# Moving the delta rule's steps in a head's plan: pairs of blocks from matmul 362 to 336, the recurrence from 400 to 374, decays loaded at 62, exponentials in four steps

## The chip, the cores and the metric

The kernel runs on one core of one Trainium2 chip. The metric is the device time of one launch in microseconds (us), lower being better. The time before is 2664.57 us, the median of 3 runs (2664.34 to 2671.64).

## What is computed

A decoder trunk of two layers over 1024 tokens and 1024 features in float32. Each layer normalises x, projects it with one large matrix, runs a sparse attention branch and a gated delta rule branch on the projections, and adds the gated mixture of the two, projected once more, to x. The part that matters here is the delta rule, for each of 8 heads, in chunks (of 64 tokens in the reference, of 128 in the kernel):

```python
decay = exp(where(incl, gc[..., :, None] - gc[..., None, :], -inf))
lower = where(strict, einsum('bhnid,bhnjd->bhnij', kb, k) * decay, 0.0)
tmat  = eye + lower
u = triangular_solve(tmat, v * beta);  w = triangular_solve(tmat, kb * exp(gc))
qk = einsum('bhnid,bhnjd->bhnij', q, k) * decay
def step(state, chunk):
    v_new = u_c - w_c @ state
    o_c   = qd_c @ state + qk_c @ v_new
    state = state * g_tot + kd_c^T @ v_new
```

q, k and v come out of a short causal convolution and a silu; the output o goes through an RMS norm and is multiplied by two gates.

## The kernel before, in words

A layer has three phases: a token phase (projections with tokens on the partitions, and the choice of keys), a feature phase (`feature_phase`, the delta rule and its gates), and attention with the output projection. Every large matmul is done as three passes over a high and a low part (`w_hi`, `w_lo`, `hi_t`, `lo_t`). The change touches the feature phase alone.

**The stream of projections.** The feature phase runs over heads 0 to 7. For each head `conv` projects k, q and v, in this order: 48 matmuls each (two halves of 24, L388). Behind each half ScalarE copies the result out (L750, L751); behind both halves VectorE does three multiply-adds of 1024 columns (L757), ScalarE a tanh (L760) and VectorE one more multiply (L761). From head 1 on, `gdn_finish` of the head before then projects two gates with 96 matmuls. So head 0 has 144 such matmuls, and each head after it 240, and `self.count` counts them over the phase (2208 in a layer, with the three gates of the attention branch that are done behind head 7's projections).

**The plan.** What is left of the delta rule is cut into small steps, and `plan_head` gives each a position: a number of projection matmuls from the head's first one. `planned` is called behind every projection matmul and emits the steps whose position has been reached. Each step's instructions are ordered behind that matmul on TensorE and behind the last evacuation (`act_last`) on ScalarE, and get a high priority; on VectorE, GpSimd and in SP's DMA queue they stand where the scheduler's order puts them. All engines run their instructions in order. A step whose data are late is moved back by the scheduler, so a position is a request. The next head starts 240 matmuls later (144 after head 0), so **position p of head h is count p − 240 of head h+1** for head 1 and later, and count p − 480 of head h+2. Head 0's positions are counts p − 144 of head 1 and p − 384 of head 2. The text below names such counts "count n".

**The steps before**, at these positions of a head:
- 80 `decays_load`: on GpSimd's queue, a DMA of 512 KB into `H` (L724), a masking sweep over it on GpSimd (affine_select, L725), then a DMA of 512 KB into `qe` (L729). `H` has two buffers, so head h+2's load waits until the last step of head h that reads `H`.
- 118 `decays_exp`: eight exponentials on ScalarE (L736).
- 100, 106 `gdn_keys`: four transposes on TensorE, a square on ScalarE (L774), a sum and a product on VectorE (L775, L787); the second half ends in a chain of small VectorE operations (L793, `rsqrt` L137 to L142, L795 to L798) that gives `g_nc`.
- 138 `gdn_row`: TensorE transposes `g_nc` (L805), ScalarE copies it (L807), and five small DMAs on SP's queue give `g_ccomp` (L809, L812).
- 142, 147 `gdn_queries`; 151 to 163 `gdn_products`: the chunks' products on TensorE (L834), each multiplied by `H` on VectorE (L836, L837); from 163 on `gdn_inverse`: DMAs out of `H` and back into `wide`, a scaling (L931), 62 small VectorE operations (L940, L942) that invert the blocks of 32, and DMAs back into `H` (L946, L949).
- 184 `qf` times `qe` (L713); 204, 210 `gdn_values`.
- 362, then every 6 matmuls: the six steps of `inverse_pairs`, which put the inverted blocks together. The first is three VectorE transposes (L959) into `xf`; the next five alternate small matmuls (L968, L975, L982, L988, L994) and their evacuations on VectorE or ScalarE, each needing the step before it.
- 400, then every 7 matmuls: the 23 steps of the recurrence, `gdn_chunks`: `g_r` (L867 on TensorE, L869 on VectorE), `g_u` (L872, then ScalarE L874), the new state `g_s` (L878, then VectorE L881 or L883) with the output (L886, L887, ScalarE L888, L890). The last read of `H` is the `g_u` of chunk 7, at position 547.
- 562 `norms` (a chain of small VectorE operations and one multiply of 1024 columns, L903 to L905) and 572, 578 `outputs` (transposes L911, a VectorE multiply L912 and a DMA each).

**One more order.** The three transposes of the pairs' first step are put behind one VectorE instruction by hand:

```python
        with self.tc.issue_after(self.convolved):     # L955; convolved is set at L757
            for b in range(3):
                nc.vector.transpose(XF[bs, :, co:co + 32], XT[bs, :, bs])
```

`self.convolved` is the last multiply-add of the latest convolution emitted by then.

Of the kernel before, what the change touches and what calls it, by code (L numbers as in the profile page):

```python
# [20 lines left out]
try:  # L21
# [10 lines left out]
OP = mybir.AluOpType  # L32
# [4 lines left out]
P = 128  # L37
S = 1024
D = 1024
T = S // P  # L40
# [29 lines left out]

AT_DECAYS, AT_EXP, AT_KEYS, AT_ROW, AT_QUERIES, AT_PRODUCTS, AT_DECAYED, AT_VALUES, AT_PAIRS, AT_CHUNKS, AT_NORMS, AT_OUTPUTS = (
    80, 118, (100, 106), 138, (142, 147), (151, 155, 159, 163), 184, (204, 210), 362, 400, 562, (572, 578))

STEP_PAIRS, STEP_CHUNKS = 6, 7

# [16 lines left out]
class Trunk:  # L94
# [207 lines left out]
    def at(self, pos, step):  # L302

        self.plan.append((pos, len(self.plan), step))
# [394 lines left out]
    def plan_head(self, p, hd, XF):  # L699

        nc = self.nc
        at = lambda pos, *steps, gap=0: [self.at(hd["at"] + pos + i * gap, f) for i, f in enumerate(steps)]
        at(AT_DECAYS, lambda: self.decays_load(p, hd))
        at(AT_EXP, lambda: self.decays_exp(hd))
        for half in range(2):
            at(AT_KEYS[half], lambda half=half: self.gdn_keys(p, hd, half))
            at(AT_QUERIES[half], lambda half=half: self.gdn_queries(hd, half))
            at(AT_VALUES[half], lambda half=half: self.gdn_values(p, hd, half))
        at(AT_ROW, lambda: self.gdn_row(p, hd))
        for i, pos in enumerate(AT_PRODUCTS):  # L710
            at(pos, lambda i=i: self.gdn_products(p, hd, 2 * i))
        at(AT_PRODUCTS[-1], lambda: self.gdn_inverse(p, hd))
        at(AT_DECAYED, lambda: nc.vector.tensor_mul(hd["qf"], hd["qf"], hd["qe"]))  # L713
        pairs = self.inverse_pairs(p, hd, XF)
        at(AT_PAIRS, *[lambda: next(pairs, None)] * 6, gap=STEP_PAIRS)
        chunks = self.gdn_chunks(p, hd)
        at(AT_CHUNKS, *[lambda: next(chunks, None)] * (3 * T - 1), gap=STEP_CHUNKS)
# [11 lines left out]
            nc.gpsimd.dma_start(out=qe.rearrange("p (t c) -> p t c", c=P),  # L729
                                in_=ap(self.rows, (T * 8 + h) * P, [[0, P], [8 * P, T], [1, P]]))  # L730

    def decays_exp(self, hd):


        for c in range(T):
            self.nc.scalar.activation(hd["H"][:, c], hd["H"][:, c], AF.Exp, bias=self.ngm[:, c, hd["h"]:hd["h"] + 1])  # L736

    def conv(self, l, p, ht, hd, name, base, bufs):

        nc = self.nc  # L740
        feat = self.feat[l]
        dst = hd[name] = p.tile([P, S], F32, name=name, bufs=bufs)
        col = base + hd["h"] * P
        cw = lambda j: feat[:, 24 * j + col // P:24 * j + col // P + 1]
        self.xps.append(self.xps.pop(0))
        xp = self.xps[0]

        def evac(hs, acc):
            o = hs.start
            nc.scalar.copy(xp[:, 4 + o:516 + o], acc)  # L750
            self.act_last = nc.scalar.activation(dst[:, hs], acc, AF.Copy, scale=cw(3)).ins  # L751

        ws = self.feat_weights(self.w_in[l], C_QKVB + col)
        for half in range(2):
            self.proj_feat(ws, half, ht, evac)
        for j in range(3):
            self.convolved = nc.vector.scalar_tensor_tensor(dst, xp[:, 1 + j:1 + j + S], cw(j), dst, op0=OP.mult,  # L757
                                                            op1=OP.add).ins
        th = xp[:, 4:4 + S]
        nc.scalar.activation(th, dst, AF.Tanh, scale=0.5)  # L760
        nc.vector.scalar_tensor_tensor(dst, th, 1.0, dst, op0=OP.add, op1=OP.mult)  # L761

    def turned(self, src, half):

# [129 lines left out]
    def gdn_finish(self, l, p, ht, hd):  # L894

        nc = self.nc
        feat = self.feat[l]
        gates = list(self.gated(l, ht, C_ZB + hd["h"] * P, C_GB + hd["h"] * P))

        def norms():  # L900
            o = hd["vb"]
            ms = self.small.tile([P, T], F32, name="g_ms")
            nc.vector.scalar_tensor_tensor(ms, hd["osq"], 1.0 / P, hd["zq"], op0=OP.mult, op1=OP.add)  # L903
            rs = self.rsqrt(ms, T)
            nc.vector.tensor_mul(o, o, rs[:, :, None].to_broadcast([P, T, P]))  # L905

        def outputs(half):
            h, b = hd["h"], gates[half]
            pt = self.tr()
            for i in range(4):  # L910
                nc.tensor.transpose(pt[:, i * P:(i + 1) * P], hd["vb"][:, 4 * half + i], self.ident)  # L911
            nc.vector.scalar_tensor_tensor(b, pt, feat[:, 96:97], b, op0=OP.mult, op1=OP.mult)  # L912
            nc.sync.dma_start(out=self.yb[h, :, 512 * half:512 * half + 512], in_=b)

        self.at(hd["at"] + AT_NORMS, norms)
        for half in range(2):
            self.at(max(hd["at"] + AT_OUTPUTS[half], self.count + 2), lambda half=half: outputs(half))
# [33 lines left out]
    def inverse_pairs(self, p, hd, XF):  # L951

        nc, nc_ = self.nc, hd["nc"]
        XT = H = hd["H"]
        with self.tc.issue_after(self.convolved):  # L955
            for b in range(3):
                bs = slice(32 * b, 32 * b + 32)
                co = 32 if b == 1 else 0
                nc.vector.transpose(XF[bs, :, co:co + 32], XT[bs, :, bs])  # L959
        yield  # L960
        ncb = lambda sl, n: nc_[sl, :, None].to_broadcast([sl.stop - sl.start, T, n])
        y2 = p.tile([P, T, 32], F32, name="y2", bufs=1)

        pairs = [(slice(32 * b, 32 * b + 32), slice(32 * b + 32, 32 * b + 64)) for b in (0, 2)]
        py = self.bank("ch")
        for c in range(T):
            for k, m in pairs:
                nc.tensor.matmul(py[m, 32 * c:32 * c + 32], H[k, c, m], XF[k, c, 0:32], start=True, stop=True)  # L968
        for k, m in pairs:
            nc.vector.tensor_mul(y2[m], py[m, :256].rearrange("p (c i) -> p c i", c=T), ncb(m, 32))  # L970
        yield
        pz = self.bank("ch")
        for c in range(T):
            for k, m in pairs:
                nc.tensor.matmul(pz[k, 32 * c:32 * c + 32], y2[m, c], XT[m, c, m], start=True, stop=True)  # L975
        for k, m in pairs:
            nc.scalar.copy(XT[k, :, m], pz[k, :256].rearrange("p (c i) -> p c i", c=T))
        yield
        m = slice(32, 64)
        pw = self.bank("ch")  # L980
        for c in range(T):
            nc.tensor.matmul(pw[m, 32 * c:32 * c + 32], XT[m, c, m], y2[m, c], start=True, stop=True)  # L982
        nc.scalar.copy(XF[m, :, 0:32], pw[m, :256].rearrange("p (c i) -> p c i", c=T))
        yield
        k, m = slice(0, 64), slice(64, 128)
        py = self.bank("ch")
        for c in range(T):
            nc.tensor.matmul(py[m, 64 * c:64 * c + 64], H[k, c, m], XF[k, c], start=True, stop=True)  # L988
        y3 = XF
        nc.vector.tensor_mul(y3[m], py[m].rearrange("p (c i) -> p c i", c=T), ncb(m, 64))  # L990
        yield
        pz = self.bank("ch")
        for c in range(T):
            nc.tensor.matmul(pz[k, 64 * c:64 * c + 64], y3[m, c], XT[m, c, m], start=True, stop=True)  # L994
        nc.scalar.copy(XT[k, :, m], pz[k].rearrange("p (c i) -> p c i", c=T))
# [252 lines left out]
```

## Time and profile before

| | |
|---|---|
| median of 3 runs | 2664.57 us (2664.34 to 2671.64) |
| the profiled execution | 2668.25 us |
| its span, first to last instruction | 2666.4 us |
| mean granted TensorE clock | 0.988 |
| TensorE busy (matmul) | 2565.7 us, 96% |
| VectorE busy | 1893.6 us, 71% |
| ScalarE busy | 1349.6 us, 51% |
| GpSimd busy | 136.1 us, 5% |
| feature phase, first layer | from 358.6 to 1066.4 us |
| feature phase, second layer | from 1675.1 to 2388.3 us |

The profile is of one execution; the sums of the prediction are made against its own 2668.25 us. A busy TensorE says that matmuls are in its pipeline, not that it works at its peak. In the rows below PE is TensorE, DVE VectorE, ACT ScalarE, POOL GpSimd, SP the queue of DMA issues. "x3" is a number of instructions, "[1.72 <-DVE ...]" the time for which the engine stood idle before the row, and what ended it.

### The profile page before, as it was taken

To read this page: it belongs to the slowest core of one execution; us is meant where nothing else is said; L and a number is where in the kernel's file an instruction comes from. 1 tells how busy PE (TensorE), PEld (TensorE's weight loads), DVE (VectorE), ACT (ScalarE), POOL (GpSimd) and SP (SyncE) were. 2 spreads that over 40 slices of the span, in tenths; PEclk is the share of its full clock that TensorE was granted. 3 is DMA by queue.
4 is the path that set the end of the run, shared out by engine and by line. 5 is a ranking of instruction groups with operands and counts; after the bars stand their busy time and mean duration, and the time that the engine had idled before them with its cause. 6 is when DMAs were issued, how large, how long until landed. Compare 5 with 4: busy or idle time off the path is not lost.

```text
span 2666.4 us, 42133 instructions
## 1 busy us (share of the span) xinstructions
PE 2565.7 (96%) x14858; PEld 2115.4 (79%) x14858; DVE 1893.6 (71%) x5086; ACT 1349.6 (51%) x3107; POOL 136.1 (5%) x382
## 2 busy tenths in 40 slices
PE   7999999999999999999999999999999999999998
PEld 7777778777888888898796777787878877878986
DVE  7677977667777853797366889776877767547965
ACT  5579734343444422797245795343444443337952
POOL 0122000000000000000001220000000000000000
PEclk9999999999999999999999999999999999999999
DMA  3122343142333323431420232422432233243233
GB/s 124 49 64 81 86 103 61 41 87 54 66 70 70 68 62 95 139 92 57 145 63 32 72 105 73 98 60 38 88 70 59 60 68 66 60 126 125 75 99 119
DMA packets 285431, 211.35 MB, mean 79 GB/s; under 512 B 72290, under 2 KB 239268, under 8 KB 285220
## 3 DMA queue, kind: packets, MB, share of 16 engines
q1 hardware_dynamic: 280612, 191.88, 25.7%
q0 software_dynamic: 4608, 16.78, 5.1%
q8 instruction: 117, 1.92, 0.3%
q14 instruction: 94, 0.77, 0.1%
HBM read 162.19 MB, written 46.40 MB: 78 GB/s over the span
## 4 chain that ended last, share of the span: by engine, by line
PE 46%; issue 20%; DVE 6%; DMA 4%; ACT 3%; POOL 1%; SPq 0%; DVEq 0%; POOLq 0%; ACTq 0%
PE acc L388 12%; PE acc L365 7%; PE more L388 5%; PE acc L1140 4%; PE wide L1108 4%; PE tr L1131 2%; PE out L365 2%; PE out L388 2%; PE tr L834 1%; ACT t_junk L596 1%; DMA H<-rows 1%; DVE t_junk L578 1%; PE wide L545 1%; DMA w_raw<-in_w_out_dram 1%; DVE scores L554 1%
## 5 line engine op out<-in xcount | busy, mean ns | idle before, releaser
L388 PE MATMUL acc<-hi_t,w_hi 128*128 128x512 f32 x1240 | 502.7, 405 | 5.6 <-DVE gate L663 5.0
L388 PE MATMUL acc<-hi_t,w_lo 128*128 128x512 f32 x1240 | 504.7, 407 | 0.0
L388 PE MATMUL acc<-lo_t,w_hi 128*128 128x512 f32 x1240 | 502.9, 406 | 0.0
L148 DVE TENSOR_TENSOR w_lo<-w_raw,w_hi 128x512 fp32r<-128x512 f32 (+1 forms) x336 | 223.6, 669 | 193.3 <-ACT w_hi L147 175.4
L147 ACT CAST w_hi<-w_raw 128x512 fp32r<-128x512 f32 (+1 forms) x336 | 201.1, 602 | 304.6 <-PE acc L388 143.4
L365 PE MATMUL acc<-w_hi,hi_t 128*128 128x512 f32 (+1 forms) x768 | 287.5, 375 | 13.7 <-ACT w_hi L147 9.0
L365 PE MATMUL acc<-w_lo,hi_t 128*128 128x512 f32 (+1 forms) x768 | 286.1, 373 | 2.2 <-DVE w_lo L148 2.2
L365 PE MATMUL acc<-w_hi,lo_t 128*128 128x512 f32 (+1 forms) x768 | 285.1, 371 | 0.0
L388 PEld LDWEIGHTS acc<-hi_t,w_hi 128*128 128x128 f32 x1240 | 234.9, 189 | 53.1 <-DVE gate L663 5.9
L388 PEld LDWEIGHTS acc<-hi_t,w_lo 128*128 128x128 f32 x1240 | 234.8, 189 | 46.4
L388 PEld LDWEIGHTS acc<-lo_t,w_hi 128*128 128x128 f32 x1240 | 234.5, 189 | 46.4
L596 ACT ACTIVATE t_junk<-scores,t_bits 128x640 f16<-128x640 f32 x248 | 198.9, 802 | 30.4 <-DVE t_bits L588 25.6
L388 PE MATMUL more<-hi_t,w_hi 128*128 128x512 f32 x488 | 198.9, 408 | 1.7 <-ACT kf L751 1.7
L388 PE MATMUL more<-hi_t,w_lo 128*128 128x512 f32 x488 | 200.3, 410 | 0.0
L388 PE MATMUL more<-lo_t,w_hi 128*128 128x512 f32 x488 | 199.2, 408 | 0.0
L365 PEld LDWEIGHTS acc<-w_hi,hi_t 128*128 128x128 f32 x768 | 146.7, 191 | 43.5 <-ACT w_hi L147 13.0
L365 PEld LDWEIGHTS acc<-w_lo,hi_t 128*128 128x128 f32 x768 | 147.2, 192 | 28.1 <-DVE w_lo L148 4.9
L365 PEld LDWEIGHTS acc<-w_hi,lo_t 128*128 128x128 f32 x768 | 147.1, 192 | 23.1 <-issue 1.0
L578 DVE TENSOR_SCALAR_CACHE_REDUCE t_junk<-scores,t_bits 128x1024 f16<-128x1024 f32 (+4 forms) x136 | 153.4, 1128 | 4.3
L874 ACT COPY g_u<-ch 128x128 f32<-128x128 f32 x128 | 33.9, 267 | 163.8 <-PE ch L872 163.6
L942 DVE TENSOR_TENSOR xc<-xc,xtmp 128x60 f32<-128x60 f32 (+24 forms) x496 | 104.9, 212 | 13.1
L940 DVE TENSOR_TENSOR xtmp<-wide,xc 128x60 f32<-128x60 f32 (+24 forms) x496 | 103.8, 209 | 11.8
(345 smaller groups left out, 5419.2 us busy)
## 6 DMA issues: line engine op xcount, KB each, us to landing
w_raw<-in_w_in_dram SPq DMA_DIRECT2D x272, 256.0 KB, 2.9
qs<-stage SPq DMA_DIRECT2D x32, 256.0 KB, 2.0
ya_gate<-gate SPq DMA_DIRECT2D x32, 256.0 KB, 3.1
H<-rows POOLq DMA_DIRECT2D x16, 512.0 KB, 8.7
qe<-rows POOLq DMA_DIRECT2D x16, 512.0 KB, 8.1
wide<-hscr SPq DMA_DIRECT2D x64, 128.0 KB, 2.6
yb<-gate SPq DMA_DIRECT2D x32, 256.0 KB, 3.7
w_raw<-in_w_out_dram SPq DMA_DIRECT2D x32, 256.0 KB, 3.8
```

The costliest lines, as they stand in the source:

```text
L147: self.nc.scalar.copy(hi, src)
L148: self.nc.vector.tensor_sub(lo, src, hi.bitcast(F32))
L365: nc.tensor.matmul(acc[t][:, :n], a[:, k, ts], ws[k][b][:, :n], start=k == 0 and i == 0, stop=k == KT - 1 and i == 2)
L388: mm = self.nc.tensor.matmul(acc, ws[k // 4][a][:, cs], act[b][:, k, hs], start=k == 0 and i == 0, stop=k == KT - 1 and i == 2)
L578: nc.vector.tensor_scalar(junk[:, :sc[i].shape[1]], sc[i], thr, 0.0, op0=op, op1=OP.add, accum_out=cnt[:, i:i + 1])
L596: nc.scalar.activation(junk[:, :n], sc[i], AF.Sign, bias=f(bits, i), scale=-1.0, accum_out=cnt[:, i:i + 1])
L874: nc.scalar.copy(u, pu)
L940: nc.vector.tensor_mul(tmp[:, :n, j + 1:], ln[:, None, j, j + 1:].to_broadcast(shape), X[:, :n, j:j + 1].to_broadcast(shape))
L942: nc.vector.tensor_add(X[:, :n, j + 1:], X[:, :n, j + 1:], tmp[:, :n, j + 1:])
L1108: nc.tensor.matmul(ps[:, :w], qt[a][:, i], kt[b][:, g, o:o + w], start=j == 0, stop=j == 2)
L1131: nc.tensor.transpose(pt[:, o:o + P], rows[i][:, j * P:(j + 1) * P], self.ident)
L1140: nc.tensor.matmul(po, a, b[:, cs], start=j == 0 and i == 0, stop=j == t and i == 2)
```

## The change

Positions in the plan: `AT_DECAYS` 80 becomes 62; `AT_EXP` 118 becomes four positions, 124, 128, 132 and 136, with two exponentials at each; `AT_ROW` 138 becomes 152; `AT_PAIRS` 362 becomes 336; `AT_CHUNKS` 400 becomes 374; `AT_NORMS` 562 becomes 537; `AT_OUTPUTS` (572, 578) become (546, 552). Keys, queries, products, the inverse, the `qf` product and the values stay where they are, and so do the distances of 6 and 7 between steps. The handle behind which the pairs' transposes are put, now `self.behind`, is the last multiply of the latest convolution (L761) or the multiply of the latest `norms` (L905), whichever was emitted last. No instruction is added or taken away.

```diff
-AT_DECAYS, AT_EXP, AT_KEYS, AT_ROW, AT_QUERIES, AT_PRODUCTS, AT_DECAYED, AT_VALUES, AT_PAIRS, AT_CHUNKS, AT_NORMS, AT_OUTPUTS = (
-    80, 118, (100, 106), 138, (142, 147), (151, 155, 159, 163), 184, (204, 210), 362, 400, 562, (572, 578))
+AT_DECAYS, AT_EXP, AT_KEYS, AT_QUERIES, AT_PRODUCTS, AT_ROW, AT_DECAYED, AT_VALUES = (
+    62, (124, 128, 132, 136), (100, 106), (142, 147), (151, 155, 159, 163), 152, 184, (204, 210))
+AT_PAIRS, AT_CHUNKS, AT_NORMS, AT_OUTPUTS = 336, 374, 537, (546, 552)
...
-        at(AT_EXP, lambda: self.decays_exp(hd))
+        for i, pos in enumerate(AT_EXP):
+            at(pos, lambda i=i: self.decays_exp(hd, 2 * i))
...
-    def decays_exp(self, hd):
+    def decays_exp(self, hd, first):
...
-        for c in range(T):
+        for c in (first, first + 1):
             self.nc.scalar.activation(hd["H"][:, c], hd["H"][:, c], AF.Exp, bias=self.ngm[:, c, hd["h"]:hd["h"] + 1])
...
-            self.convolved = nc.vector.scalar_tensor_tensor(dst, xp[:, 1 + j:1 + j + S], cw(j), dst, op0=OP.mult,
-                                                            op1=OP.add).ins
+            nc.vector.scalar_tensor_tensor(dst, xp[:, 1 + j:1 + j + S], cw(j), dst, op0=OP.mult, op1=OP.add)
         th = xp[:, 4:4 + S]
         nc.scalar.activation(th, dst, AF.Tanh, scale=0.5)
-        nc.vector.scalar_tensor_tensor(dst, th, 1.0, dst, op0=OP.add, op1=OP.mult)
+        self.behind = nc.vector.scalar_tensor_tensor(dst, th, 1.0, dst, op0=OP.add, op1=OP.mult).ins
...
-            nc.vector.tensor_mul(o, o, rs[:, :, None].to_broadcast([P, T, P]))
+            self.behind = nc.vector.tensor_mul(o, o, rs[:, :, None].to_broadcast([P, T, P])).ins
...
-        with self.tc.issue_after(self.convolved):
+        with self.tc.issue_after(self.behind):
```

## Rows read from the trace of the kernel before

**Rows 1.** The two feature phases, busy time by engine (PE, PEld, DVE, ACT, POOL).

```profile
358.60:1066.40 707.80, 690.32 (x4219) 563.90 (x4218) 488.37 (x1294) 276.78 (x713) 23.96 (x25) 0.99 0.34 70
1675.10:2388.30 713.20, 694.07 (x4219) 566.58 (x4218) 488.90 (x1295) 276.10 (x712) 23.29 (x25) 0.99 0.31 69
```

**Rows 2.** Waits of TensorE: us in total, times, longest us.

```profile
PE ch L968 <- DVE rs_t L140: 14.9, 8, 3.5
...
PE ch L878 <- ACT g_u L874: 9.9, 2, 5.0
...
PE tr L805 <- DVE xtmp L940: 4.5, 2, 3.0
...
PE tr L805 <- DVE g_nc L796: 2.7, 2, 1.4
```

**Rows 3.** One steady head, head 4 of the first layer, all its 240 matmuls.

```profile
644.90:723.10 78.20, 76.48 (x493) 63.21 (x492) 58.44 (x155) 32.92 (x87) 2.83 (x3) 1.00 0.35 67
```

**Rows 4.** TensorE in that head, in order of time: start us, us, instruction.

```profile
680.32 0.40 PE L388 MATMUL more<-lo_t,w_hi 128*128 128x512 f32 x1
680.56 0.39 PE L388 MATMUL more<-hi_t,w_lo 128*128 128x512 f32 x1
682.67 0.21 PE L968 MATMUL ch<-xf,H 32*32 32x32 f32 x2 [1.72 <-DVE rs_t L140]
```

**Rows 5.** VectorE in that head.

```profile
672.47 1.40 DVE L912 SCALAR_TENSOR_TENSOR gate<-tr,feat,gate 128x512 f32<-128x512 f32 x2
673.80 2.04 DVE L757 SCALAR_TENSOR_TENSOR qf<-xp,feat,qf 128x1024 f32<-128x1024 f32 x1
676.88 0.69 DVE L775 TENSOR_REDUCE g_ssq<-th 128x4 f32<-128x512 f32 x1 [1.04 <-ACT th L774]
...
680.82 1.28 DVE L757 SCALAR_TENSOR_TENSOR qf<-xp,feat,qf 128x1024 f32<-128x1024 f32 x1
...
682.10 0.43 DVE L959 STREAM_TRANSPOSE xf<-H 32x256 f32<-32x256 f32 x1
```

**Rows 6.** ScalarE in that head.

```profile
674.79 1.57 ACT L736 ACTIVATE H<-H,ngm 128x128 f32<-128x128 f32 x5 [1.88 <-POOL H L725]
676.27 0.58 ACT L774 ACTIVATE th<-tr 128x512 f32<-128x512 f32 x1
```

**Rows 7.** GpSimd in that head.

```profile
664.81 0.88 POOL L724 DMA_DIRECT2D H<-rows  x1 [69.44 <-ACT g_u L874]
673.66 1.09 POOL L725 TENSOR_SCALAR_AFFINE_SELECT H<-H 128x1024 f32<-128x1024 f32 x1 [7.97 <-DMA H<-rows]
```

**Rows 8.** SP's issue of the inverted blocks in that head, and the landing of all such DMAs.

```profile
661.18 1.82 SPq L949 DMA_DIRECT2D H<-xscr  x4
...
DMA to landing us min/median/max: 1.8/1.8/2.7
```

**Rows 9.** Its stretches 671.9:682.7, 682.7:693.4 and 693.4:702.4 together (counts 96 to 169).

```profile
sum 30.50, PE 28.78 PEld 23.34 DVE 26.52 ACT 13.87 POOL 1.95; mean PE 9.59 PEld 7.78 DVE 8.84 ACT 4.62 POOL 0.65
```

**Rows 10.** The row's transpose on TensorE, heads 0 and 3 of the first layer.

```profile
395.99 0.27 PE L805 MATMUL tr<-ident,g_nc 128*8 128x128 f32 x1 [1.33 <-DVE g_nc L796]
...
606.01 0.27 PE L805 MATMUL tr<-ident,g_nc 128*8 128x128 f32 x1 [3.02 <-DVE xtmp L940]
```

**Rows 11.** Stretches at half the clock (PEclk last but two), and the sum of three such.

```profile
2153.60:2163.80 10.20, 10.20 (x99) 7.20 (x98) 4.59 (x16) 2.77 (x8) 0.00 (x0) 0.50 0.11 27
...
sum 17.10, PE 17.10 PEld 12.61 DVE 10.37 ACT 3.58 POOL 0.00; mean PE 5.70 PEld 4.20 DVE 3.46 ACT 1.19 POOL 0.00
```

**Rows 12.** Head 2 of the first layer: ScalarE, then TensorE.

```profile
544.93 2.44 ACT L736 ACTIVATE H<-H,ngm 128x128 f32<-128x128 f32 x8 [5.67 <-POOL H L725]
...
547.58 0.80 PE L878 MATMUL ch<-g_u,kdec 128*128 128x128 f32 x2 [4.92 <-ACT g_u L874]
```

**Rows 13.** VectorE groups of the steady head: operation and count, then busy us, mean ns.

```profile
L869 DVE SCALAR_TENSOR_TENSOR g_r<-ch,g_nce,vb 128x128 f32<-128x128 f32 x8 | 2.8, 346 | 1.3 <-PE ch L867 1.2
...
L905 DVE TENSOR_TENSOR vb<-vb,rs_y 128x1024 f32<-128x1024 f32 x1 | 1.2, 1224 | 0.0
```

## The prediction
> **What bounds the kernel now.** First I read how the phases fill TensorE: in the two feature phases, which are all that the change touches, it is busy for 690 of 708 us and 694 of 713 us [rows 1]. So nothing is to be had but its idle time, some 37 us together, and what idle time brings with it. Next the list of TensorE's waits: four kinds in the feature phase are worth a microsecond or more at a time [rows 2]. Eight times the pairs' first matmul waits, 14.9 us in all. Four times the transpose of the row waits, 4.5 and 2.7 us. Twice the recurrence waits 5 us for a `g_u`. Then one steady head in order of time. Heads 4 to 7 of both layers look alike: 240 matmuls take 78.2 us, of which TensorE is busy for 76.48 [rows 3], and the whole rest is one stall of 1.72 us before the pairs' first matmul at count 128 [rows 4].
>
> How that stall comes about is seen by following it back through the engines. The pairs' transposes on VectorE run at 682.10, right behind the third multiply-add of q's convolution [rows 5], because the order by hand puts them there. That multiply-add is late: VectorE first stood idle for 1.04 us, waiting for ScalarE's square of the keys (L774) [rows 5], and the square stood behind five exponentials, which in turn waited 1.88 us for GpSimd's sweep over `H` [rows 6]. The sweep ended at 674.75, because `H` was loaded only at 664.81, when head 2's last `g_u` had freed the buffer, and took 8.8 us to come [rows 7]. So ScalarE is parked on a slow load while the keys stand behind it, VectorE runs late, and TensorE pays.
>
> **The change, part by part.** Durations are those of the profiled execution, 2668.25 us; that is 3.7 us above the median of 2664.57.
>
> *Load and exponentials.* The last read of `H` moves with the recurrence from count 67 to count 41, 26 matmuls earlier. At 0.24 us from one start to the next [rows 4], and with recurrence steps between, that is some 7.5 us. GpSimd's queue holds only the load, the sweep and the `qe` load, and starts when the buffer is free. So the sweep would end at about 667 in place of 674.75, and the exponentials, now ordered behind v's first evacuation at count 120, find `H` ready. ScalarE's wait of 1.88 us goes in ten heads (3 to 7 of two layers), and the keys' squares no longer stand behind it. What it costs: 2.44 us of exponentials [rows 12] move to counts 124 to 136, two at a time (0.7 us), beside the pairs' last copy and the first `g_u`. A step of the recurrence has 7 matmuls, 1.7 us, for its answer; I take 0.
>
> *Pairs at count 96 in place of 122.* Their data are there: the inverted blocks are sent back to `H` from 661.18 to 663.0 and land 1.8 us later [rows 8], near count 68. The new handle puts the transposes behind the norms' multiply, which now starts from count 57, in place of q's convolution. So VectorE can do them at count 96, before q's first multiply-add has its input. The stall at 128 goes: −14.9 us, with 0 as the other end. Late next would be the pairs' second step, a VectorE product that finds a multiply-add of 1.28 us running; six matmuls and the keys' transposes, over 1.4 us, lie between, and I take 0.
>
> *Row at 152 in place of 138.* Fourteen matmuls more, over 3 us, against waits of 1.33 us in head 0 and 3.02 us in head 3 of the first layer [rows 10]: all four go, −7.2 us (the other end is 0). Its five DMAs pass one weight load on SP and are done well before `g_ccomp` is used at count 209, so nothing waits for them.
>
> *Norms and outputs 25 and 26 earlier.* They leave the crowded stretch: two products of 1.4 us together [rows 5] and 1.2 us of norms [rows 13] now fall between counts 57 and 90, where the recurrence has ended at 55. TensorE is asked for the outputs' transposes at counts 66 and 72 and may wait for the norms.
>
> *The sweep's new place.* In the steady head q's first multiply-add took 2.04 us in place of 1.28 while the sweep ran beside it [rows 5, 7], 0.76 us more. At its new time, near count 78, the sweep meets k's last multiply or the norms' multiply, with the outputs' transposes waiting. Bounds 0 and 0.76 us in each of ten heads; without a row that is nearer, I take the middle, 3.8 us. The Trainium skill, SBUF — State Buffer, "Who interferes with whom", has a rule that speaks against this move: of a VectorE operation with two SBUF inputs and a GpSimd operation that reads SBUF, the later one blocks until the first has ended. By it the multiply-add that began 0.14 us into a sweep of 1.09 would have lost 0.95 us, where the row shows 0.76; an estimate from the rule would put 9.5 us in place of 3.8, and the sum at 2650.
>
> *The recurrence in the crowded stretch.* Its first steps now lie at counts 134 to 160, beside v's convolution and the products. VectorE is busy for 26.5 of 30.5 us between counts 96 and 169 [rows 9]; the change takes some 2.2 us out of it (outputs, the sweep's 0.76) and puts one microsecond of `g_s` and `g_r` in. A `g_r` takes 0.35 us [rows 13]; behind a running multiply-add of 1.28 and a matmul of 0.27 it answers in 1.9 us, where 7 matmuls give 1.6: 0.3 us late. I take one such per head in ten heads, +3 us. The bounds are 0 and, with all four VectorE steps behind one whole multiply-add, 5.1 us a head.
>
> *Clock.* Three stretches of 17.1 us in all ran at half the clock (granted 0.50, that is 1.2 of 2.4 GHz), each after one of these stalls [rows 11]; six of the eight pairs' stalls brought none. At half rate half of that is lost: −8.5 us, other end 0. The median lies below this execution by about what the longest of them cost.
>
> *Head 2 of each layer.* ScalarE waits 5.67 us in front of the exponentials and TensorE 4.92 us for the `g_u` queued behind them [rows 12]. There `H` is freed by head 0's recurrence, which is held up by head 1's pairs and those by head 1's inverse, and the pairs and the recurrence keep their distance to each other (106 matmuls): I take no change, with 9.9 us as the other end.
>
> The sum: 2668.25 − 14.9 − 7.2 − 8.5 + 3.8 + 3.0 = **2644.5 us**, 0.75% below the median. The profile can tell a change from none beyond about 0.3%, 8 us: below 2656.6 or above 2672.6.
>
> **The rivals.**
>
> *A, the stall only moves.* VectorE is as busy as before between counts 96 and 130, now with the pairs' three evacuations among q's multiply-adds, so TensorE waits there instead. For it: VectorE has 4 us free of 30.5 there [rows 9]. Against it: in the steady head the wait for ScalarE alone explains the delay. Then only the row's 7.2 us are gained and 3 lost: 2664, no change. Chance 0.17.
>
> *B, the plan is not kept.* A position is a request, and a step whose data are late is moved back. If the scheduler leaves the pairs of the steady heads near count 122, nothing happens but the row: 2661 to 2668. Against it, data 28 counts early [rows 8]. Chance 0.05.
>
> *C, head 2's stalls go too.* If the four small groups of exponentials let `g_u` pass between them, 9.9 us more go [rows 2]: 2634.6. Against it: the load of `H` there is no earlier. Chance 0.10.
>
> *D, slower.* The recurrence's four VectorE steps at counts 141 to 169 queue behind the convolution, 1.28 us each, and TensorE, in order, waits each time: 5.1 us a head, 51 us in ten heads: 2644.5 − 3.0 + 51 = 2692. It decides from 3.1 us a head, where the time passes 2672.6. For it: 86% busy in this stretch. Against it: before, the pairs' evacuations lay in the same stretch, and TensorE did not wait there. Chance 0.13.
>
> **How the numbers follow.** The forecast has 0.55. Faster by over 0.3%: forecast and C, 0.65, and a little of A where part of the stall goes, 0.66. Within 0.3%: the rest of A and B, 0.21. Slower: D, 0.13. The range runs from 2628, which is C with the sweep and the recurrence at nothing (6.8 us less), to 2668, the upper end of B; it leaves out D and little else.
>
> **What would show it.** Right: steady heads of 76.5 to 77 us; no wait of L968; ScalarE's L736 without a wait for GpSimd in heads 3 to 7; the load of `H` 7 us earlier against the head's first matmul; L805 gone from the waits; head 2's waits as before. Wrong: waits of L975 or L988 for VectorE (A), L959 still at count 128 (B), or L872 and L867 among the longest waits (D).

## The result, and the profile after

Measured side by side on one chip, the changed kernel took 2652.13 us (median of 20 executions, 2638.25 to 2669.51) and the kernel before 2670.98 us (20 executions, 2662.16 to 2685.04): a ratio of **0.9936, with a 95% interval of 0.992 to 0.9952**, 0.64% faster. The forecast of 2644.5 us was 0.75% below the median known then. The profiled execution took 2649.04 us, 19.2 less than the 2668.25 of before, where the sum had 23.8 less. The total is about right. What it is made of is not, and that is what the experiments are about.

In the changed kernel the lines lie one or two further down from L388 on: L388 is L389, L724 to L729 are L726 to L731, L736 is L738, L768 is L769, L805 is L806, L874 and L878 are L875 and L879, L905 and L912 are L906 and L913, L946 to L968 are L947 to L969.

First the two feature phases of the kernel after and, below them, heads 4 and 5 of the first layer (they answer to [rows 1, 3]). The columns are start:end, length, busy time of PE, PEld, DVE, ACT and POOL, granted clock, share of DMA, GB/s.

```profile
361.90:1066.70 704.80, 689.77 (x4220) 564.16 (x4219) 489.33 (x1295) 276.85 (x715) 27.83 (x25) 0.99 0.34 72
1674.40:2376.70 702.30, 689.45 (x4220) 563.43 (x4219) 489.78 (x1296) 276.85 (x715) 27.60 (x25) 0.99 0.32 73
...
643.20:719.30 76.10, 76.10 (x492) 63.03 (x491) 55.45 (x144) 32.46 (x87) 3.72 (x3) 1.00 0.34 70
719.30:797.00 77.70, 76.45 (x493) 62.98 (x492) 58.19 (x158) 32.56 (x87) 3.81 (x3) 1.00 0.35 67
```

The phases are 3.0 and 10.9 us shorter. Head 4, 78.2 us before, now takes 76.1 and TensorE is busy throughout. Head 5, which should look the same, has 1.25 us without work in it. The waits of TensorE, kernel after (they answer to [rows 2]; us in total, times, longest us), show what that is:

```profile
PE tr L769 <- DVE gate L913: 11.3, 4, 5.6
PE ch L879 <- ACT g_u L875: 9.8, 2, 5.0
...
PE tr L912 <- DVE vb L906: 3.8, 6, 1.3
...
PE ch L976 <- DVE y L971: 0.9, 4, 0.2
...
PE tr L769 <- DVE qf L762: 0.5, 2, 0.3
```

The pairs' wait (14.9 us) and the row's (7.2) are gone, and head 2's wait for `g_u` stands as it stood. But there is a **new wait, now the largest of the feature phases**: the keys' transposes (L769) wait for the outputs' multiply (L913), 11.3 us in four heads. So the change cleared 22.1 us of stalls and made one of half that size.

The largest of the four, from the second half of head 6 to head 7 of the first layer, followed through the queues and engines of the kernel after. GpSimd and SP's queue first (start us, us, instruction; for a DMA the time is that of its issue):

```profile
886.07 0.88 POOL L726 DMA_DIRECT2D H<-rows  x1 [64.08 <-ACT g_u L875]
895.39 1.09 POOL L727 TENSOR_SCALAR_AFFINE_SELECT H<-H 128x1024 f32<-128x1024 f32 x1 [8.44 <-DMA H<-rows]
896.43 0.91 POOL L731 DMA_DIRECT2D qe<-rows  x1
...
887.53 2.51 SPq L947 DMA_DIRECT2D xscr<-xc  x4
890.14 0.55 SPq L331 DMA_DIRECT2D w_raw<-in_w_in_dram  x1
896.28 1.83 SPq L950 DMA_DIRECT2D H<-xscr  x4
```

then VectorE and TensorE:

```profile
895.49 2.07 DVE L906 TENSOR_TENSOR vb<-vb,rs_y 128x1024 f32<-128x1024 f32 x1
898.09 0.43 DVE L960 STREAM_TRANSPOSE xf<-H 32x256 f32<-32x256 f32 x1 [0.54 <-DMA H<-xscr]
899.09 0.43 DVE L960 STREAM_TRANSPOSE xf<-H 32x256 f32<-32x256 f32 x1 [0.57 <-DMA H<-xscr]
905.82 0.44 DVE L960 STREAM_TRANSPOSE xf<-H 32x256 f32<-32x256 f32 x1 [6.30 <-DMA H<-xscr]
906.29 1.41 DVE L913 SCALAR_TENSOR_TENSOR gate<-tr,feat,gate 128x512 f32<-128x512 f32 x2
...
907.10 1.12 PE L769 MATMUL tr<-ident,kf 128*128 128x128 f32 x4 [5.59 <-DVE gate L913]
```

The inverse sends its blocks to memory (`xscr`, four DMAs of 32 KB, L947) and fetches them back into the layout of `H` (L950). The fetch waits for the sending to land. The two together are called the round trip below, and its time is taken from the issue of the sending to the issue of the fetch. Here it is issued 8.75 us after it (887.53 to 896.28), and the last block arrives just before 905.8, 7.7 us after the last of the four issues (898.1), in place of 1.8 [rows 8]. VectorE, in order, stands 6.30 us in front of the third transpose of the pairs. Behind it stand the outputs' two multiplies, and they hold the buffer `tr` that the keys' transposes want, so TensorE stops for 5.59 us.

The late issue of the fetch goes with the first line: GpSimd's load of 512 KB into `H` was issued 1.46 us before the inverse's DMAs. In the kernel before the sending was issued at 656.59, 4.59 us ahead of the fetch at 661.18 [rows 8], and the load only at 664.81 [rows 7]:

```profile
656.59 2.52 SPq L946 DMA_DIRECT2D xscr<-xc  x4
...
674.71 0.91 POOL L729 DMA_DIRECT2D qe<-rows  x1
```

The late landing is another matter, for `H` had been loaded when its sweep began at 895.39. What goes out then is GpSimd's second load of 512 KB, `qe`, at 896.43, 0.15 us behind the fetch's first DMA; in the kernel before it went out at 674.71, 13.5 us behind the fetch. The other long stall of this trace is of the same kind, while in head 5, where `qe` goes out 1.17 us behind the fetch, TensorE waits for 1.03 us only:

```profile
2133.82 1.83 SPq L950 DMA_DIRECT2D H<-xscr  x4
2134.01 0.91 POOL L731 DMA_DIRECT2D qe<-rows  x1
2141.55 1.00 PE L769 MATMUL tr<-ident,kf 128*128 128x128 f32 x4 [4.49 <-DVE gate L913]
...
742.24 2.72 SPq L950 DMA_DIRECT2D H<-xscr  x4
743.41 0.91 POOL L731 DMA_DIRECT2D qe<-rows  x1
747.49 0.66 PE L769 MATMUL tr<-ident,kf 128*128 128x128 f32 x4 [1.03 <-DVE gate L913]
```

These two stalls are 10.1 of the 11.3 us. In the three traces that have the early load (this one, a second one of the changed kernel, and that of the pairs and the recurrence alone) 20 round trips meet it. In five of them `qe` went out 0.15 to 0.32 us behind the fetch's first DMA, and TensorE waited 4.5 to 5.6 us; in the other 15 it went out 0.57 to 1.41 us behind, and the wait was 0 to 1.6 us. So the load of `H` makes the fetch late, and the long stalls come where the `qe` load then meets the fetch. No run moves one of the two loads without the other, so this division is read from the traces and not tested.

The effect on the sending is seen in the sums too. SP's fetch waits 10.7 us over the whole kernel before (first line) and 37.3 us after (second fence); the DMA share between the sending and the fetch (last column but one) was 0.49 before and is 0.83 after.

```profile
SPq L949 <- DMA xscr<-xc: 10.7, 13, 2.6
...
659.20:661.10 1.90, 1.90 (x13) 1.67 (x12) 1.62 (x3) 1.49 (x5) 0.00 (x0) 1.00 0.49 85
```

```profile
SPq L950 <- DMA xscr<-xc: 37.3, 14, 6.6
...
890.10:896.20 6.10, 6.10 (x27) 4.91 (x27) 5.79 (x15) 2.59 (x4) 0.81 (x1) 1.00 0.83 112
```

Heads 3 and 7 of the same trace are a control (a head is here the one whose blocks are sent, while the next head is projected). In head 3 the load comes 2.8 us after the sending, in head 7 there is none near, and the fetch of both is issued after 4.0 us. In heads 4 to 6 of both layers, where the load is 1.5 us ahead, that takes 8.7 to 9.9 us.

Last, half clock. The stretch behind the longest stall in the kernel after (clock in the last column but two):

```profile
905.90:912.80 6.90, 5.70 (x47) 4.50 (x48) 5.78 (x9) 0.60 (x1) 0.00 (x0) 0.51 0.53 154
2141.60:2145.10 3.50, 3.50 (x40) 2.69 (x41) 3.50 (x6) 0.60 (x1) 0.00 (x0) 0.52 0.73 210
```

Each follows one of the two longest new stalls: 10.4 us at 1.2 GHz, where two of the pairs' stalls and one of the row's had brought 17.1 [rows 11]. Head 2's two stretches of 6.8 us are in both kernels. How many of these stalls an execution has differs: a second profile of the changed kernel shows two, 6.0 us in all, and a span of 2635.1 in place of 2647.3. What decides seems to be small: in three of the five long stalls GpSimd's sweep over `H` began 0.01 to 0.10 us ahead of the norms' multiply and took 1.09 us, so that `qe`, behind it, met the fetch; where the sweep began just behind the multiply it took some 2 us, and `qe` missed it. This is a likely reason for the width of 2638 to 2669 us; it was not tested.

### The profile page after: what moved, and what is told of

The parts are those of the page before. It is cut to its first block, busy times and chain, and to the rows that moved or that the text cites. A ratio compares the mean times of both kernels' runs of the same rounds, so it can differ in the third digit from the quotient of the medians.

```text
span 2647.3 us, 42080 instructions
## 1 busy us (share of the span) xinstructions
PE 2561.8 (97%) x14858; PEld 2115.1 (80%) x14858; DVE 1894.2 (72%) x5086; ACT 1347.3 (51%) x3107; POOL 144.2 (5%) x382
## 4 chain that ended last, share of the span: by engine, by line
PE 62%; DVE 11%; DMA 5%; ACT 3%; issue 2%; SPq 1%; POOL 0%; DVEq 0%; ACTq 0%
PE acc L389 19%; PE more L389 9%; PE acc L366 7%; PE acc L1141 4%; PE wide L1109 4%; PE tr L1132 2%; PE out L366 2%; PE tr L835 2%; PE out L389 2%; DVE xc L943 1%; DVE xtmp L941 1%; DVE w_lo L149 1%; PE tr L769 1%; ACT t_junk L597 1%; DMA xscr<-xc 1%
## 5 line engine op out<-in xcount | busy, mean ns | idle before, releaser
L389 PE MATMUL acc<-hi_t,w_hi 128*128 128x512 f32 x1240 | 504.3, 407 | 5.1 <-DVE gate L664 5.1
L389 PE MATMUL acc<-lo_t,w_hi 128*128 128x512 f32 x1240 | 502.9, 406 | 0.0
L389 PE MATMUL acc<-hi_t,w_lo 128*128 128x512 f32 x1240 | 501.3, 404 | 0.0
L389 PEld LDWEIGHTS acc<-hi_t,w_hi 128*128 128x128 f32 x1240 | 234.7, 189 | 53.3 <-DVE gate L664 5.9
L389 PEld LDWEIGHTS acc<-hi_t,w_lo 128*128 128x128 f32 x1240 | 234.9, 189 | 48.4
L389 PEld LDWEIGHTS acc<-lo_t,w_hi 128*128 128x128 f32 x1240 | 235.1, 190 | 46.3
L389 PE MATMUL more<-hi_t,w_hi 128*128 128x512 f32 x488 | 200.0, 410 | 0.5 <-ACT kf L753 0.5
L389 PE MATMUL more<-lo_t,w_hi 128*128 128x512 f32 x488 | 199.1, 408 | 0.0
L389 PE MATMUL more<-hi_t,w_lo 128*128 128x512 f32 x488 | 198.8, 407 | 0.0
L555 DVE SCALAR_TENSOR_TENSOR scores<-relu,w_idx,scores 128x384 f32<-128x384 f32 (+5 forms) x84 | 80.9, 963 | 40.6 <-ACT relu L548 34.0
```

The lines of the kernel that those rows point to most:

```text
L389: mm = self.nc.tensor.matmul(acc, ws[k // 4][a][:, cs], act[b][:, k, hs], start=k == 0 and i == 0, stop=k == KT - 1 and i == 2)
L555: nc.vector.scalar_tensor_tensor(sc[:, :n], rel[half][:, :n], wc, sc[:, :n], op0=OP.mult, op1=OP.add)
```

## The experiments

All ratios are against the kernel before, timed on the same chip in the same set of runs; the kernel before had a median of 2671.85 us in the first set (the first four), 2675.1 in the second and 2671.84 in the third.

**Exponentials alone**, in the kernel before:

```diff
-    80, 118, (100, 106), 138, (142, 147), (151, 155, 159, 163), 184, (204, 210), 362, 400, 562, (572, 578))
+    80, (124, 128, 132, 136), (100, 106), 138, (142, 147), (151, 155, 159, 163), 184, (204, 210), 362, 400, 562, (572, 578))
...
-        at(AT_EXP, lambda: self.decays_exp(hd))
+        for i, pos in enumerate(AT_EXP):
+            at(pos, lambda i=i: self.decays_exp(hd, 2 * i))
...
```

> The kernel before with one part of the change alone: exponentials in four steps at 124, 128, 132, 136; pairs, recurrence, row and load stay. Theory (the stall at count 128 comes from exponentials parked in front of the keys on ScalarE): ScalarE no longer waits for GpSimd in heads 4 to 7, the keys' squares run at once, and the eight stalls before L968 fall from 14.9 us to under 5; time 0.4% below before. Rival (it is the pairs' place among q's multiply-adds that makes the stall): the waits of L968 stay near 15 us and the time is that of before.

2645.8 us, ratio 0.9904 [0.988, 0.9928]. Its waits of TensorE:

```profile
PE tr L1037 <- DVE kt_lo L148: 4.3, 2, 2.3
PE tr L806 <- DVE g_nc L797: 2.0, 3, 1.0
PE ch L969 <- DVE rs_t L140: 1.4, 4, 0.4
```

The pairs' wait falls from 14.9 to 1.4 us with the pairs where they were. The chain read in the prediction (exponentials park ScalarE, the keys' square is late, VectorE is late) is shown by its own cure. The gain is more than twice the 0.4% expected: the row's waits fall with it, from 7.2 to 2.9 us in all, and the half clock behind the pairs' and the row's stalls is gone. The load still comes 6.5 us or more after the inverse's sending, and the round trip stays at 4.0 us in most heads. As far as the two intervals can tell, this part alone gains at least as much as the whole change (0.9936 [0.992, 0.9952]).

**Row alone**, in the kernel before:

```diff
-    80, 118, (100, 106), 138, (142, 147), (151, 155, 159, 163), 184, (204, 210), 362, 400, 562, (572, 578))
+    80, 118, (100, 106), 152, (142, 147), (151, 155, 159, 163), 184, (204, 210), 362, 400, 562, (572, 578))
```

> The kernel before with the row at 152 in place of 138, nothing else. Theory: the four waits of L805, 7.2 us, are gone and nothing replaces them; L968 still waits 15 us; time 0.25% below before. Rival (the row was only the first to meet a late VectorE): as much appears in front of the queries' or products' matmuls, and the time is that of before.

2669.45 us, ratio 0.9993 [0.9975, 1.0011]: no difference that can be told. The row's 7.2 us of waits go, and 3.1 come back in another place:

```profile
PE ch L968 <- DVE rs_t L140: 17.1, 8, 3.0
...
PE tr L768 <- DVE qf L761: 3.1, 4, 1.4
```

The queries' transposes, which are now ahead of the row's on TensorE, wait for VectorE in the row's place, and in this execution the pairs waited 2.2 us longer.

**Pairs, recurrence, norms and outputs alone**, in the kernel before (with the new handle):

```diff
-    80, 118, (100, 106), 138, (142, 147), (151, 155, 159, 163), 184, (204, 210), 362, 400, 562, (572, 578))
+    80, 118, (100, 106), 138, (142, 147), (151, 155, 159, 163), 184, (204, 210), 336, 374, 537, (546, 552))
...
+            self.behind = nc.vector.tensor_mul(o, o, rs[:, :, None].to_broadcast([P, T, P])).ins
...
+        with self.tc.issue_after(self.behind):
...
```

> The kernel before with pairs at 336, recurrence at 374, norms and outputs at 537, 546, 552 and the new handle; exponentials stay in one step at 118, the row at 138, the load at 80. Theory: H is free 26 matmuls earlier whatever AT_DECAYS says, so its load starts at count 41 to 42 as in the changed kernel, ScalarE does not wait in heads 4 to 7, the stalls before L968 go, the row's 7 us stay, and the keys' transposes at count 99 wait some 11 us where H's load meets the inverse's DMAs; time 0.3% to 0.4% below before. Rival (the four steps are what matters): the exponentials at 118 still hold the keys back, and 10 us or more are lost to them at L968 or at the keys.

2653.66 us, ratio 0.9937 [0.9915, 0.9959]. The new stall is there without the exponentials, the row or the load's new position:

```profile
PE tr L767 <- DVE gate L911: 13.7, 5, 5.5
...
PE tr L910 <- DVE vb L904: 4.8, 6, 1.3
PE tr L804 <- DVE g_nc L795: 3.9, 3, 2.0
```

`AT_DECAYS` stands at 80 here, and in heads 4 to 6 the load still comes at least 1.5 us ahead of the sending: its time is set by the buffer that the earlier recurrence frees, not by its position. The round trips there are 8.4 to 9.5 us. In head 3 the load comes 0.7 us behind the sending, and they are the longest of all, 10.8 and 12.6 us.

**Load kept behind the inverse**, in the changed kernel: from head 3 on a copy on GpSimd that reads the `H` of the head before, and so waits for its inverted blocks, stands ahead of the load. This is called the gate below; it holds back the `qe` load too, which follows the load of `H` in GpSimd's queue.

```diff
+            if h >= 3:
+                seen = self.small.tile([P, 4], F32, name="g_seen")
+                read = nc.gpsimd.tensor_copy(seen, self.inverted[:, 0, 0:P:32])
+                ctx.enter_context(self.tc.issue_after(read.ins))
             nc.gpsimd.dma_start(out=E, in_=ap(self.rows, h * P, [[0, P], [8 * P, T], [1, P]]))
+        self.inverted = E
```

> The changed kernel, but from head 3 on a small copy on GpSimd reads the head before's H, which the inverse's last DMAs write, and the load of H stands behind it: it starts only when the inverted blocks have landed. Theory (H's load and the inverse's DMAs share the DMA engines and the blocks land 5 us late): the time from the issue of xscr to the issue of H<-xscr is 4 us in every head in place of 9 in heads 4 to 6, the waits of L769 for the outputs' multiplies (11.3 us) fall under 2 us, the half clock behind them goes, and the time is 0.3% to 0.5% below the changed kernel, some 1.0% below before. Rival (the new handle holds the transposes behind late norms): the waits of L769 stay near 11 us and the time is that of the changed kernel.

2642.3 us, ratio 0.9892 [0.9869, 0.9915]. The wait at the keys' transposes is gone, the round trips of heads 4 to 6 are back at 4.0 us (4.85 once), and from the keys of one of the heads behind them to those of the next it is 76.1 us. What it pays is in heads 3 and 4, where the inverse is later and the load, waiting for it, is late itself:

```profile
PE tr L841 <- DVE H L844: 3.4, 2, 2.2
PE ch L879 <- ACT H L1002: 3.2, 2, 1.7
```

**The changed kernel again**, beside the next three:

> The changed kernel itself, as the measure for the others on this chip. All theories: 0.6% below before; waits of L769 for the outputs' multiplies of some 10 us, differing from execution to execution.

2655.85 us, ratio 0.9936 [0.9908, 0.9964], the first result again.

**Exponentials and row**, in the kernel before (both edits above):

> The kernel before with exponentials in four steps and the row at 152; pairs, recurrence and load stay. Theory (these two parts bring the gain; the earlier pairs and recurrence only bring the collision of H's load with the inverse's DMAs): L805 waits 2 us less than with the four steps alone, L968 waits 2 us or less, H's load starts 6.5 us behind xscr, and the time is 0.3% to 0.5% below the changed kernel, 1.0% below before. Rival (the earlier pairs are needed): no faster than the changed kernel.

2644.38 us, ratio 0.9894 [0.9865, 0.9922]. No wait at L806 is left, and L969 keeps 2.2 us. It is not told apart from the exponentials alone.

**Pairs early, recurrence not**, in the changed kernel:

```diff
-    62, (124, 128, 132, 136), (100, 106), (142, 147), (151, 155, 159, 163), 152, 184, (204, 210))
-AT_PAIRS, AT_CHUNKS, AT_NORMS, AT_OUTPUTS = 336, 374, 537, (546, 552)
+    80, (124, 128, 132, 136), (100, 106), (142, 147), (151, 155, 159, 163), 152, 184, (204, 210))
+AT_PAIRS, AT_CHUNKS, AT_NORMS, AT_OUTPUTS = 336, 400, 562, (572, 578)
```

> The changed kernel with the recurrence, norms and outputs back at 400, 562, 572 and 578, and the load at 80; pairs stay at 336. H is then free, and its load starts, 6.5 us behind xscr. Theory (the collision comes from the earlier recurrence, not from the earlier pairs): xscr to H<-xscr takes 4 us, L769 does not wait for the outputs' multiplies, L968 does not wait, and the time is about that of exponentials and row alone, 1.0% below before. Rival (the pairs at 336 are too early in any case): TensorE waits 8 us or more at the pairs' matmuls or the keys, and the time is that of the changed kernel.

2642.89 us, ratio 0.9893 [0.9868, 0.9917]. The pairs stay at 336, and neither wait is there: none of L969, none of L769 for L913. The load comes 5.8 us after the sending, the fetch after 4.0 us (4.8 and 5.0 in two heads), and head 5 takes 76.5 us. So the early pairs do no harm there; the early recurrence does, through the buffer that it frees. In head 2 there is another wait:

```profile
PE tr L835 <- DVE H L838: 9.6, 2, 5.0
```

The products' transposes stop for about as long as the recurrence did for its `g_u`, and that wait is gone. ScalarE still stands for 5.07 us in the first layer in front of the exponentials of head 2's `H`, waiting for the sweep. So head 2's stall has only changed its place, which points to its late `H`.

**Load kept behind the inverse from head 4 on**: the gate above with `if h >= 4`.

> As the kernel in which H's load stands behind the landing of the inverted blocks, but from head 4 on in place of head 3. There the load of head 3 waited for head 2's late inverse, and TensorE lost some 7 us at the products and the recurrence of head 3 and at the recurrence of head 4. Theory: these waits go, L769 still does not wait, and the time is 0.1% to 0.2% below that kernel, 1.2% below before. Rival (GpSimd's extra wait costs as much wherever it is): the same time as with head 3.

2631.79 us, ratio **0.9852 [0.9826, 0.9877]**: more than the 1.2% expected, though the interval meets that of the gate from head 3 on. SP's queue and GpSimd in head 5 of the first layer:

```profile
731.11 2.52 SPq L953 DMA_DIRECT2D xscr<-xc  x4
733.72 0.55 SPq L331 DMA_DIRECT2D w_raw<-in_w_in_dram  x1
735.05 1.82 SPq L956 DMA_DIRECT2D H<-xscr  x4
...
738.40 0.19 POOL L729 COPY g_seen<-H 128x4 f32<-128x4 f32 x1 [67.99 <-ACT qf L759]
738.90 0.88 POOL L731 DMA_DIRECT2D H<-rows  x1 [0.32 <-issue]
748.18 1.09 POOL L733 TENSOR_SCALAR_AFFINE_SELECT H<-H 128x1024 f32<-128x1024 f32 x1 [8.40 <-DMA H<-rows]
```

The fetch follows the sending by 3.94 us, the blocks land by 738.4, and only then does the load go out; its sweep at 748.18 is still ahead of the exponentials. The largest waits left in the feature phases:

```profile
PE ch L885 <- ACT g_u L881: 10.2, 2, 5.1
...
PE tr L918 <- DVE vb L912: 3.3, 4, 1.3
```

The gate is all that separates this from the changed kernel beside it (0.9936 [0.9908, 0.9964]): 0.84%, some 22 us, with intervals that do not meet. So the early time of GpSimd's loads costs at least about as much as the whole gain that was measured. That it is their meeting with the round trip rests on the traces: the round trips of heads 4 to 6 are back at 4 us (5.0 once), and the wait of L769 for the outputs' multiplies is gone. The two profiled spans differ by 21.4 us (2647.3 and 2625.9), and 20.0 of them lie where the gate acts, between the sendings of heads 0 and 7: 513.2 and 509.8 us in the changed kernel, 501.6 and 501.4 here. The trace of the changed kernel shows 11.3 us of it as waits and 5.2 as half clock (half of 10.4); the rest was not followed, and executions differ in it. This is also the fastest version of the study, ahead of both kernels.

**The same again, and an attempt on head 2.** The attempt puts head 2's exponentials 86 positions later, its products and inverse 67 and its `qf` product 47 later:

```diff
+        late = hd["h"] == 2
-            at(pos, lambda i=i: self.decays_exp(hd, 2 * i))
+            at(pos + 86 * late, lambda i=i: self.decays_exp(hd, 2 * i))
...
+            at(pos + 67 * late, lambda i=i: self.gdn_products(p, hd, 2 * i))
...
```

> The gated version from head 4 on once more, unchanged, for comparison on the same chip. If its 0.985 of before was the gate's doing, it comes again within 0.983 to 0.988, under the changed kernel's 0.9936 by 0.6 to 1 per cent. If it was one lucky set of executions, it comes out near the version gated from head 3 on, 0.989 or more.

> The gated version from head 4 on, and in head 2 of each layer the exponentials 86 matmuls later, the products and the inverse 67 later and the qf product 47 later. Theory: in head 2 ScalarE stands parked for 5 us on exponentials whose H is not yet loaded, with head 1's g_u behind them; placed behind the load they park nothing, so the two waits of the recurrence for g_u (10.2 us in the gated version) go, and with them some half clock: 10 to 14 us below the gated version beside it, about 0.980 of before. Rival: head 2 is late because its buffer of H is late, and whatever is put later there is missed later: the products and the inverse end later, the pairs and the recurrence of head 2 wait for them, and head 3 loses as much as head 2 gains: 0.985, with waits of 3 us or more at the pairs' first transposes or the values in heads 2 and 3.

The repetition gave 2629.56 us, 0.9842 [0.982, 0.9863], within the range expected if the gate was the reason. The attempt gave 2641.59 us, 0.9891 [0.9871, 0.9911], slower than what it started from. The theory's figure missed, and the rival had the direction right but not the reason, for the stall in head 2 did not go at all. ScalarE in the attempt, head 2 of the first layer:

```profile
536.57 0.20 ACT L898 ACTIVATION_READ_ACCUMULATOR o_junk<-oc 128x1 f32 x1
542.64 0.69 ACT L745 ACTIVATE H<-H,ngm 128x128 f32<-128x128 f32 x2 [5.86 <-POOL H L734]
543.24 0.24 ACT L882 COPY g_u<-ch 128x128 f32<-128x128 f32 x1
```

It stands 5.86 us in front of the first two exponentials, with a `g_u` behind them. Position 210 did not hold these back from a place ahead of the `g_u` of about count 200; the likely reason is that on ScalarE a step is ordered only behind the last evacuation, and that of count 192 lies before both. The products and the inverse did come later, and the recurrence of head 3 pays for it (5.6 us of waits for the pairs' last copy). So head 2's stall is not settled here: that its exponentials stand in front of `g_u` is shown, that it can be had away with a gain is not.

## Why the prediction was right and wrong

**Right: the chain and the pairs' stall.** The term of −14.9 us came in full. But one part would have done: by the exponentials' own run, moving them takes 13.5 of the 14.9 us away, with the pairs and the load left in place. The prediction gave the two edits one result each ("ScalarE's wait goes", "the stall at 128 goes") and did not ask whether the second was still needed behind the first.

**The step that failed: "Their data are there", at count 68, and "GpSimd's queue holds only the load, the sweep and the `qe` load".** The landing of the blocks was taken from a trace in which the loads of `H` and `qe` came after it, and they were moved by 7.5 us without being looked at against the inverse's DMAs. The load of `H` moved as forecast: 19.9 us behind its head's first matmul before (664.81 − 644.90), 12.6 us after in head 5 (731.86 − 719.30). That put it 1.5 us ahead of the sending, where it had been 6.5 us or more behind it, and `qe` beside the fetch. GpSimd's queue was checked for what stands in it, and the transfers under way from SP's queue at the same time were not. The price, 11.3 us of waits at L769, was in no term and in no rival. Rival A had the stall only move, but to other instructions and for another reason.

**The row: −7.2.** All four waits went, and 0.5 us came back at the queries' transposes (L769 for `qf` L762). Alone, the step is worth nothing that can be told. The prediction's other end of 0 was the better value for it.

**The sweep: +3.8.** The wait of the outputs' transposes for the norms' multiply is 3.8 us in six heads, against 0.4 in two before. That this is the forecast's figure is luck. In two of the six heads alone the multiply began behind a sweep (2.07 and 2.01 us in place of 1.22), and the waits there are 0.75 and 0.68 us, 1.4 together. In the version gated from head 4 on no multiply runs beside a sweep, and 3.3 us of these waits are left (L918 for L912). The estimate by the Trainium skill's rule, 9.5 us, is not borne out as a loss of time, though the pairs of instructions do behave nearly as that rule says (SBUF — State Buffer, "Who interferes with whom"). In head 7 the multiply began 0.10 us behind a sweep of 1.09 and took 2.07 us in place of 1.22; with a full wait it would be 2.21. In head 5 it was the sweep that came second:

```profile
741.28 1.22 DVE L906 TENSOR_TENSOR vb<-vb,rs_y 128x1024 f32<-128x1024 f32 x1
...
741.38 2.07 POOL L727 TENSOR_SCALAR_AFFINE_SELECT H<-H 128x1024 f32<-128x1024 f32 x1 [8.64 <-DMA H<-rows]
```

There GpSimd paid in VectorE's place, and `qe`, behind the sweep, went out 1.17 us behind the fetch and not 0.15. The estimate had VectorE second in all ten heads.

**The recurrence in the crowded stretch: +3.0.** The list of waits has none of L868 or L873; the pairs' second evacuation, costed at 0, shows 0.9 us (L976). So the 3.0 us were not paid. Rival D did not occur (its "86%" is 87%, 26.5 of 30.5 us).

**Clock: −8.5.** Half-clock stretches went from 17.1 us to 10.4, and half of the difference, 3.3 us, is gained, because the new stall brings them as the old one did.

**Head 2: 0.** 9.9 us before, 9.8 after, as argued; rival C did not occur.

**A gain not seen: −4.7.** The keys' transposes of the attention branch, at the end of each feature phase (L1036), waited 4.7 us for VectorE before and do not wait after. Head 7's recurrence and outputs now end earlier there. The wait stays in every run with the recurrence at 400 (3.0 to 4.6 us) and is at most 0.2 us in the ones with it at 374.

**The account.** In the feature phases −14.9 − 7.2 + 11.3 + 0.5 + 3.4 + 0.9 = −6.0 us of waits and −3.3 of clock make 9.3 of the 13.9 us by which they are shorter; the other 4.6 are small waits that the prediction did not name, or are not assigned. The rest of the kernel is 5.2 us shorter: the stretch ahead of the first phase is 3.3 us longer, those behind the two phases are 1.0 and 7.5 us shorter, and the keys' transposes are 4.7 us of these. So the total came near the forecast by luck: 11.3 us of waits that were in no term and 5.2 us of clock that did not come stand against the recurrence's 3.0 that were not paid and gains that no term had.

## What to carry to other kernels

A step that frees a buffer earlier starts a transfer earlier, and those queued behind it. Look at which other transfers they then meet, in all queues and not in their own alone, above all a small round trip through memory that someone waits for. And when two edits cure the same stall, time each alone: here the exponentials alone gained as much as all the edits together, and the whole did better (0.985 against 0.990) only once the load was held back by a gate.

## What the runs showed of the hardware that was not expected

A round trip of four DMAs of 32 KB through memory, whose second half is issued 4.0 us behind its first in most heads, takes 8.4 to 9.9 us to that point when a load of 512 KB was issued 1.5 to 1.8 us ahead of it, 10.8 and 12.6 us with the load 0.7 us behind it, and still 4.0 us with the load 2.8 us behind it. The second half, which lands 1.8 us behind its issue when nothing meets it, landed 4.6 to 7.7 us behind its last issue (by the transpose that waited for it) in the five cases where another 512 KB load went out 0.15 to 0.32 us behind its first. That it is the DMA engines' shared time, and not the memory or the reading of `rows` 128 times over, was not told apart.
